# Attention outputs stored as high and low sums and added in the gating step, staging tiles laid out by last use, norm loads moved ahead, a minimum folded into the scores' reduction, and a dense store of the last block

## The chip, the cores and the metric

The kernel runs on one core of a Trainium2 chip. A core has a matrix engine (TensorE, PE in the profile; its weight loads are listed as PEld), three engines for elementwise work (VectorE is DVE, ScalarE is ACT, GpSimd is POOL), a queue that issues transfers (SyncE, SP), and 16 DMA engines between the chip's memory and the on-chip memory (SBUF; matmuls write to the accumulator memory, PSUM). The metric is the device time of one execution in microseconds (us), lower is better; three timed runs of the kernel before have a median of 1828.3 us (1823.72 to 1830.45).

## What is computed

Two layers over 2048 prompt frames and 32 frames of a second group, model width 1024, all in float32. Layer 0 is windowed attention in two kinds of head (A: 8 query heads that share 2 key/value heads, with sinks; B: 8 heads over a band of 9 chunks with a bias), each output gated by SiLU; layer 1 is a gated linear recurrence.

```python
for l in range(DEPTH):
    hp = rms_norm(yp, ln_pre[l])                      # and the same for the 32 frames
    if l % 2 == 0:
        qa, ka, va, ga, qb, kb, vb, gb = ab_project(hp, pos_p, w_in_ab[j])
        oa = prompt_band(qa, ka, va, N_PREV_A, None, sinks_a[j])
        ob = prompt_band(qb, kb, vb, N_PREV_B, relpos_b[j], None)
        mp = concatenate([oa * silu(ga), ob * silu(gb)]) @ w_out_ab
    else:
        mp = lru_mixer(hp, ...)       # in-projection, width-4 conv, gates, scan, out-projection
    yp = yp + rms_norm(mp, ln_post[l])
```

## The kernel before

**Numbers in two parts.** A float32 value is split into a high part that a fast matmul takes exactly and a low part, the rest. A dense product runs three matmuls for each 128 x 128 weight tile: high x high, high weight x low, low weight x high (`mm_list`). Attention's values are stored with the high part in columns 0 to 63 and the low part in columns 64 to 127 of one 128-wide tile, so that the product P V leaves the high sums on partitions 0 to 63 and the low sums on 64 to 127 of PSUM, and the two halves have to be added.

**Tiling.** The 2084 columns (2048 frames, 4 of padding, 32) are six blocks of 352 (the last has 324), taken in pairs b = 0, 1, 2; everything lies transposed, features on partitions. `dense_P` runs the input projection of layer 0: for each pair 26 weight tiles, each over both blocks. Its results are finished by small routines (`fin_ka`, `fin_q1`, `fin_v`, `fin_kq`, `fin_z`) that put keys, queries, values and gates into scratch tensors in the chip's memory. Attention runs beside it as units of 128 queries: `soft` does the scores, the minimum of their negative and the exponential, `transp` transposes the probabilities and splits them, then P V goes to the one tile of the ring `Or`. `evac_O` and `evac_B` bring that to SBUF (ScalarE copies one half, VectorE adds the other half to it; a head of kind B sums two more partial sums) and store it in the scratch tensor `oT` [1024, 2084]. `y_proc` loads `oT` and the gates `zT`, multiplies them and splits the product into `r0h`/`r0l` (pairs 0 and 2) or `r1h`/`r1l` (pair 1). From there `out_part` runs the output projection; its results pass `fin_out` (scale, squares, sum over features, reciprocal root, residual), into a tile `m`, and to `x2T`. Layer 1 then runs for each pair `norm_proc` (load `x2T`, norm, split), `in_part` (16 weight tiles with conv, gates and scan) and `out_part`; the last one writes the output `yT`.

**What sets the order.** The program is written out by a list scheduler inside the kernel (`Sched`, a cost for each operation, priorities in `spawn`). Each routine is a generator that yields a request (`R`) with the engine, what must be ready, and rings from which it wants tiles; where it asks for `("V", "G")` the scheduler takes VectorE or GpSimd, whichever it expects to finish first. So an edit in one routine reorders all engines behind it. After attention `sch.alone` keeps GpSimd out of most work.

**Places that the change touches.** `soft` (a row of up to 640 scores lies in two PSUM tiles, each reduced by one VectorE instruction into a column of `nm`, and a third instruction, `tensor_tensor(nm, nm, min)`, joins the two columns before the exponential); `evac_O`, `evac_B`; `y_proc` (12 quarter-block columns of 176, two half-feature loads each, ready for `out_part` a block at a time); the pool `stg` of staging tiles (`s`, `sr`, `vst`, `xcs`, `r0b`), whose place in SBUF is taken by the pool `mp` (`m`, `sacc`, `r`, `tz`) when the input projection is done, a new tile waiting for the last use of the ones under it; `dense_2`, which starts `norm_proc` of the next pair after `in_part`; `fin_out` with `res_load` for the last block, in two pieces of 162 columns, VectorE and GpSimd sharing the work.

Of the kernel before, what the change touches and what calls it, by code (L numbers as in the profile page):

```python
# [52 lines left out]
WIN = 3.4133  # L53

# [344 lines left out]
def hybrid_kernel(ctx, tc, I, O):  # L399
# [30 lines left out]
    oT, zT, x2T = dt("oT", [D, TOK]), dt("zT", [D, TOK]), dt("x2T", [D, TOK])  # L430
# [129 lines left out]
    def late_consts():  # L560
# [6 lines left out]
        SP.dma_start(out=oT[:, SEQ:S0].rearrange("(k p) t -> p k t", p=128), in_=zpad)  # L567
# [47 lines left out]
    def subs(blk):  # L615
        w = BW[blk] // 2
        return [(0, w), (w, w)]
# [46 lines left out]
    def norm_proc(src, b, gi, ri, key, rings, free=None, after=None, src_ready=(), then=None, blocks=(0, 1)):  # L664
# [119 lines left out]
    def y_proc(b, ri, key, free=None, then=None):  # L784

        hh, hl = RT[ri]
        todo = [(bi, t0, col, w, 4 * j) for bi, t0, col, w in cells_of(b) for j in range(2)]
        cur = {}

        def y_load():  # L790
            for n, (_, t0, _, w, k0) in enumerate(todo):
                g = xrr if b == 0 and n % 3 == 2 else xtr
                x, = yield R("SP", [("o", min(b + 1, 2)), ("z", b)], [g])
                for j, src in enumerate((oT, zT)):
                    SP.dma_start(out=x[:, 4 * j:4 * j + 4, :w],
                                 in_=src[k0 * 128:k0 * 128 + 512, t0:t0 + w].rearrange("(k p) t -> p k t", p=128))
                cur[n] = x, g
                sch.set((key, "x", n))
        spawn(y_load(), PY if b == 0 else PY2)
        for n, (bi, t0, col, w, k0) in enumerate(todo):  # L800
            yield R("V", [(key, "x", n)])
            x, g = cur[n]
            o = x[:, 0:4, :w]
            e, _ = yield R(("V", "G"), [x], cost=(0.8, 1.63))
            ENG[e].tensor_tensor(o, o, x[:, 4:8, :w], OP.mult)
            ks, cs = slice(k0, k0 + 4), slice(col, col + w)
# [5 lines left out]
            g.release(x)  # L812
            if n % 4 == 3:
                sch.set((key, bi), max(sch.t["V"], sch.t["G"]) + 0.13)
# [32 lines left out]
    sr = ring(sp, [128, BLK], "s", 7)  # L847
    srr = ring(sp, [128, 2, BLK], "sr", 3, F32R)
    hlr.append(srr)
    vsr = ring(sp, [128, 3, 2, 128], "vst", 1, F32R)  # L850

    xcr = ring(sp, [128, KT, 176], "xcs", 1)
    xct = {}
    ctn = {}
    r0[1] = sp.tile([128, BLK], F32, name="r0b", tag="r0b")
# [318 lines left out]
    otr = Ring(sch, ap, [128, 512], F32, "ot", 2, halves=True)  # L1174
# [56 lines left out]
    def soft(run, np_, groups, out, sink=None):  # L1231
# [10 lines left out]
        def reduce(ps, pieces, o0):  # L1242
            yield R("V", [ps] + ex)
# [7 lines left out]
            Sr.release(ps)  # L1251
            left[0] -= 1
# [9 lines left out]
        for gi, pieces in enumerate(groups):  # L1262
# [10 lines left out]
            spawn(reduce(ps, pieces, o0), PT)  # L1273
# [41 lines left out]
    def evac_O(b, ps, n, dst, view=None, beside=False):  # L1315

        m = 2 * n if beside else n
        ot, = yield R("A", [ps], [otr])
        x = ot.start_partition()
        A.copy(ot[:, :m], ps[64 - x:128 - x, :m])  # L1320
        yield R("V", [ot])
        V.tensor_tensor(ot[:, :m], ps[x:x + 64, :m], ot[:, :m], OP.add)
        Or.release(ps)
        if beside:
            yield R("V", [ot])
            V.tensor_tensor(ot[:, :n], ot[:, :n], ot[:, n:m], OP.add)
        yield R("SP", [ot])
        SP.dma_start(out=dst, in_=view(ot) if view else ot[:, :n])
        o_done(b, ot)

    def o_done(b, ot):
        otr.release(ot)
# [3 lines left out]

    def evac_B(b, ps, dst, i0):

        ot, = yield R("A", [ps], [otr])
        x = ot.start_partition()  # L1340
        v = ps.rearrange("p (i x c) -> p i x c", i=2, x=2)
        o = ot.rearrange("p (x i c) -> p i x c", i=2, x=2)
        A.copy(o[:, i0:], v[64 - x:128 - x, i0:])
        if i0:
            A.copy(o[:, 0, 1], v[64 - x:128 - x, 0, 1])
        yield R("V", [ot])
        V.tensor_tensor(o[:, i0:], v[x:x + 64, i0:], o[:, i0:], OP.add)
        if i0:
            V.tensor_tensor(o[:, 0, 1], v[x:x + 64, 0, 1], o[:, 0, 1], OP.add)
        Or.release(ps)  # L1350
        yield R("V", [ot])
        V.tensor_tensor(o[:, i0:, 1], o[:, i0:, 0], o[:, i0:, 1], OP.add)
        yield R("SP", [ot])
        SP.dma_start(out=dst, in_=ot[:, 256:512])
        o_done(b, ot)
# [4 lines left out]
    def run_B(b, h, tiles):  # L1360
# [7 lines left out]
        def unit(t):  # L1368
# [6 lines left out]
            def proc(run):  # L1375
# [35 lines left out]
                yield from evac_B(b, po, oT[512 + h * 64:512 + h * 64 + 64, ta * 128:ta * 128 + 256], 2 - len(edges))  # L1411
# [710 lines left out]
```

## Time and profile before

The profile is one execution, taken with every instruction's start and duration. It says:

| | |
|---|---|
| time of the profiled execution | 1823.5 us |
| its span, first to last instruction | 1821.7 us |
| median of three timed runs | 1828.3 us (1823.72 to 1830.45) |
| TensorE busy / VectorE / ScalarE / GpSimd | 95% / 85% / 55% / 18% of the span |
| DMA engines | 66.5% of 16, 362.80 MB, 199 GB/s |
| mean granted TensorE clock | 0.988 of full speed |
| matmuls of the dense projections | some 325 ns each, one starting about every 160 ns |

"Busy" counts an engine from an instruction's start to its end. Matmuls overlap: one is 320 ns under way, and the next starts 160 ns after it. So a PE that is idle in the records has had no matmul under way at all, and shorter delays between starts don't show as idle time. A row of a group gives engine, operation, output <- inputs, shape and count, then the summed time and the mean of one in ns, then the idle time of the engine just ahead of them and whose end closed it. All rows carry the line of one helper (L101), so groups are told apart by their tiles.

### The profile page before, as it was taken

The page shows a single profiled execution, that of the slowest core. Times are in us where ns is not written, and L with a number is a line of the kernel's source. Part 1 is how long each engine was busy: PE and PEld are TensorE (multiplying, and loading weights), DVE is VectorE, ACT ScalarE, POOL GpSimd, SP SyncE. Part 2 cuts the span into 40 slices and gives each one's busy share as a digit, 9 for nine tenths or more (in the row PEclk, how much of TensorE's full clock was granted, in tenths as well). Part 3 has the DMA queues.
Part 4 walks back from the last instruction along what each step waited for, and adds up shares of the span by engine and source line. Part 5 has one row for each costly group of instructions (what it writes and reads, how often), then busy time and mean ns, then how long its engine had stood idle before and what let it go on. Part 6 is the DMA issues. An engine that isn't in the chain of part 4 may idle for free.

```text
span 1821.7 us, 31694 instructions
## 1 busy us (share of the span) xinstructions
PE 1731.5 (95%) x11078; PEld 1671.8 (92%) x11078; DVE 1555.3 (85%) x3330; ACT 996.5 (55%) x2037; POOL 326.5 (18%) x284
## 2 busy tenths in 40 slices
PE   8999999999999999999998999998999999999995
PEld 7999999998999999899997999998999899999995
DVE  9899967899998779998988789899999988798843
ACT  4275543476666416665565344457753675447831
POOL 4332204323322233311222000000011000100002
PEclk8999999999999999999998999999999999999998
DMA  5788766888654368877764985684566735575376
GB/s 179 203 245 265 228 190 196 226 232 237 192 149 141 97 186 248 210 217 195 216 194 122 278 248 168 210 267 147 217 213 217 204 124 174 165 208 171 128 268 193
DMA packets 293576, 362.80 MB, mean 199 GB/s; under 512 B 36308, under 2 KB 244616, under 8 KB 293400
## 3 DMA queue, kind: packets, MB, share of 16 engines
q1 hardware_dynamic: 293416, 360.78, 66.5%
q8 instruction: 87, 1.43, 0.3%
q14 instruction: 73, 0.60, 0.1%
HBM read 255.77 MB, written 107.00 MB: 199 GB/s over the span
## 4 chain that ended last, share of the span: by engine, by line
PE 49%; DVE 29%; DMA 9%; ACT 6%; issue 4%; SPq 1%; POOL 1%; DVEq 0%; ACTq 0%; POOLq 0%
PE acc L101 35%; PE T L101 4%; PE O L101 4%; PE S L101 4%; DVE pt L101 3%; DVE ex L101 3%; DVE m L101 3%; DMA xr<-x2T 3%; DVE ss L101 2%; DVE ti L101 2%; DVE xs L101 2%; DVE s L101 2%; DVE pp L101 2%; DVE eti L101 1%; DVE wl L101 1%
## 5 line engine op out<-in xcount | busy, mean ns | idle before, releaser
L101 PE MATMUL acc<-r0h,wh 128*128 128x352 f32 (+2 forms) x1832 | 592.1, 323 | 6.7 <-ACT tzb L101 2.9
L101 PE MATMUL acc<-r0h,wl 128*128 128x352 f32 (+2 forms) x1832 | 592.2, 323 | 2.9 <-DMA wl<-wo1s 2.9
L101 PE MATMUL acc<-r0l,wh 128*128 128x352 f32 (+2 forms) x1832 | 592.5, 323 | 0.6 <-DVE r0l L101 0.5
L101 PEld LDWEIGHTS acc<-r0h,wh 128*128 128x128 f32 x1832 | 346.2, 189 | 9.3 <-ACT tzb L101 3.1
L101 PEld LDWEIGHTS acc<-r0h,wl 128*128 128x128 f32 x1832 | 346.3, 189 | 4.8 <-DMA wl<-wo1s 4.0
L101 PEld LDWEIGHTS acc<-r0l,wh 128*128 128x128 f32 x1832 | 346.4, 189 | 2.2 <-DVE r0l L101 1.2
L101 PE MATMUL acc<-r1h,wh 128*128 128x352 f32 (+1 forms) x864 | 277.5, 321 | 5.2 <-ACT tz L101 3.6
L101 PE MATMUL acc<-r1h,wl 128*128 128x352 f32 (+1 forms) x864 | 277.0, 321 | 1.6 <-DVE wl L101 1.6
L101 PE MATMUL acc<-r1l,wh 128*128 128x352 f32 (+1 forms) x864 | 276.9, 321 | 0.0
L101 ACT ACTIVATE pt<-pt,nm 128x256 f32<-128x256 f32 (+6 forms) x272 | 169.8, 627 | 61.2 <-DVE nm L101 59.3
L101 ACT CAST pp<-T 128x256 fp32r<-128x256 f32 (+4 forms) x314 | 134.0, 438 | 84.3 <-PE T L101 65.8
L101 PEld LDWEIGHTS acc<-r1h,wh 128*128 128x128 f32 x864 | 162.3, 188 | 6.4 <-ACT tz L101 4.5
L101 POOL TENSOR_SCALAR pt<-pt,rr 128x256 f32<-128x256 f32 (+4 forms) x142 | 100.2, 716 | 366.4 <-DVE rr L101 217.0
L101 PEld LDWEIGHTS acc<-r1h,wl 128*128 128x128 f32 x864 | 162.3, 188 | 1.9 <-DVE wl L101 1.9
L101 PEld LDWEIGHTS acc<-r1l,wh 128*128 128x128 f32 x864 | 162.3, 188 | 0.0
L101 PE MATMUL T<-ident,pt 128*128 128x128 f32 (+2 forms) x864 | 143.3, 274 | 18.0 <-DVE pp L101 10.2
L101 DVE TENSOR_TENSOR pp<-T,pp 128x256 fp32r<-128x256 f32 (+4 forms) x314 | 150.4, 496 | 7.9 <-ACT pp L101 6.0
L101 PE MATMUL O<-pp,vt 128*128 128x256 f32 (+3 forms) x728 | 135.9, 310 | 9.8 <-DVE pp L101 4.7
L101 PEld LDWEIGHTS T<-ident,pt 128*128 128x128 f32 (+2 forms) x864 | 101.7, 140 | 42.4 <-DVE pp L101 19.9
L101 DVE CUSTOM_DVE_ANT_0 pt<-S,bias 128x320 f32<-128x320 f32 (+2 forms) x240 | 108.8, 478 | 17.4 <-PE S L101 14.6
L101 PE MATMUL S<-kk,qa 128*128 128x320 f32 (+5 forms) x376 | 119.7, 333 | 3.8 <-DVE nm L101 3.3
L101 PEld LDWEIGHTS O<-pp,vt 128*128 128x128 f32 (+1 forms) x728 | 107.1, 193 | 16.0 <-DVE pp L101 6.1
(241 smaller groups left out, 3010.1 us busy)
## 6 DMA issues: line engine op xcount, KB each, us to landing
wst<-w_in SPq DMA_DIRECT2D x93, 512.0 KB, 4.4
wst<-wo_in SPq DMA_DIRECT2D x32, 512.0 KB, 5.6
wh<-w1s SPq DMA_DIRECT2D x32, 512.0 KB, 3.8
wl<-w1s SPq DMA_DIRECT2D x32, 512.0 KB, 4.6
wh<-wo1s SPq DMA_DIRECT2D x24, 512.0 KB, 3.9
wl<-wo1s SPq DMA_DIRECT2D x24, 512.0 KB, 4.7
kk<-kB SPq DMA_DIRECT2D x32, 320.0 KB, 4.8
vt<-vB SPq DMA_DIRECT2D x16, 640.0 KB, 4.8
```

The lines of the kernel that those rows point to most:

```text
L101: r = fn(*a, **k)
```

## The change

1. `oT` gets 2048 rows: high and low sums are stored as they come. `evac_O` (heads A) only copies on ScalarE, in two 128 x 256 pieces. `evac_add` (heads B and the 32 frames) adds the two partial sums at all 128 partitions, once. The add of high and low moves to `y_proc`, which now goes by two feature tiles of a whole block (352 columns): two loads of 64 partitions bring high and low side by side, one 128 x 704 add, one multiplication, copy and split, and a key for each feature tile, so that `out_part` can begin with the first.
2. The pool `stg` is laid out `r0b`, `vst`, `xcs`, `sr`, `s`; the second tile of `m` becomes `mb` and lies last in `mp`.
3. `norm_proc` of the next pair starts before `in_part`, loads at once, and holds its ScalarE work until `in_part` is written out.
4. The second reduction of a pair takes the first one's column of `nm` as its starting value, and the joining instruction goes.
5. The last block is finished in pieces of 176, 64 and 84 columns, its last matmuls split 240 + 84, all on VectorE, added into the residual's tile, and stored to a new output `yL` in which each partition's columns lie together; the host puts it in place.

```diff
-    oT, zT, x2T = dt("oT", [D, TOK]), dt("zT", [D, TOK]), dt("x2T", [D, TOK])
+    oT, zT, x2T = dt("oT", [2 * D, TOK]), dt("zT", [D, TOK]), dt("x2T", [D, TOK])
...
         early = len(rings) == len(idx)
         for i, g in zip(idx, rings):
             yield from load(i, g)
+        if hold:
+
+            yield R("A", [hold])
...
     def y_proc(b, ri, key, free=None, then=None):
-        todo = [(bi, t0, col, w, 4 * j) for bi, t0, col, w in cells_of(b) for j in range(2)]
+        todo = [(bi, T0[2 * b + bi], BW[2 * b + bi], k) for bi in range(2) for k in range(0, KT, 2)]
...
+                x, = yield R("SP", [("o", min(b + 1, 2))], [xtr])
+                for j in range(2):
+                    r = k * 256 + j * 256
+                    SP.dma_start(out=tile4(x)[j * 64:j * 64 + 64, :, :w], in_=oT[r:r + 256, t0:t0 + w].rearrange("(s d) t -> d s t", s=4))
...
             e, _ = yield R(("V", "G"), [x], cost=(0.8, 1.63))
-            ENG[e].tensor_tensor(o, o, x[:, 4:8, :w], OP.mult)
+            ENG[e].tensor_tensor(o, o, v[:, :, 1], OP.add)
+            th = sch.t[e] + 0.13
+            e, _ = yield R(("V", "G"), [lambda: th, z], cost=(0.8, 1.63))
+            ENG[e].tensor_tensor(o, o, tile4(z)[:, k % 4:k % 4 + 2, :w], OP.mult)
...
-            if n % 4 == 3:
-                sch.set((key, bi), max(sch.t["V"], sch.t["G"]) + 0.13)
+            for c in range(k, k + 2):
+                sch.set((key, bi, c), sch.t[e] + 0.13)
...
+                if sink is None:
+                    j = len(groups) - 1 - gi
                 V.tensor_tensor_reduce(out=pt[:np_, o0 + o:o0 + o + n], in0=ps[:np_, o:o + n], in1=bv, scale=-1.0,
-                                       scalar=BIG if sink is None else nsk[:np_, sink + j:sink + j + 1],
+                                       scalar=nsk[:np_, sink + j:sink + j + 1] if sink is not None else nm[:np_, 1:2] if on else BIG,
                                        op0=OP.add, op1=OP.min, accum_out=nm[:np_, j:j + 1])
...
-                if sink is None and len(groups) == 2:
-                    V.tensor_tensor(nm[:np_, 0:1], nm[:np_, 0:1], nm[:np_, 1:2], OP.min)
...
+    def evac_O(b, ps, g, t0):
+
+        for i in range(2):
+            ot, = yield R("A", [ps], [otr])
+            A.copy(ot, ps[:, i * 256:i * 256 + 256])
+            if i:
+                Or.release(ps)
+            yield R("SP", [ot])
+            SP.dma_start(out=o_two(g, i, t0, 128), in_=ot.rearrange("p (j n) -> p j n", j=2))
...
-        V.tensor_tensor(ot[:, :m], ps[x:x + 64, :m], ot[:, :m], OP.add)
-            V.tensor_tensor(ot[:, :n], ot[:, :n], ot[:, n:m], OP.add)
...
+            V.tensor_tensor(o2[:, i0:], v1[:, i0:], o2[:, i0:], OP.add)
...
-    mr, sar, r2r = ring(mp, [128, KT, BLK], "m", 2), ring(mp, [128, BLK], "sacc", 2), ring(mp, [128, BLK], "r", 1)
+    mr = ring(mp, [128, KT, BLK], "m", 1)
+    sar, r2r = ring(mp, [128, BLK], "sacc", 2), ring(mp, [128, BLK], "r", 1)
...
+                if half:
+
+                    V.tensor_tensor(xt[:, ks], m[:, ks, cc], xt[:, ks], OP.add)
+                    th = sch.t[e] + 0.13
+                    yield R("SP", [lambda: th])
+                    SP.dma_start(out=O["yL"][:, KT * o + ks.start * sw:KT * o + ks.stop * sw].rearrange("p (k t) -> p k t", t=sw), in_=xt[:, ks])
...
-                for o, sw in subs(2 * b + bi):
+                for o, sw in ((0, LAST[2][0]), LAST[2]):
```

Counted over the whole program, PE's matmuls stay as they are but for the last block's split; VectorE goes from 3314 to 3194 instructions, GpSimd from 255 to 207, ScalarE from 1672 to 1685, and SP from 1227 to 1277 transfers. The order is the same up to the first output of attention, some 98 us into the span. Three places on VectorE show what moved.

VectorE inside attention, before: the second reduction of a row of scores (ISA, from the score tile `S` with the bias into `pt` and the column `nm`), its read-out, the joining of the columns, and an output of a B head between them (`ot` from PSUM tile `O`, later `ot` with itself):

```order
L101 ISA pt_210,nm_216<-S_195,bias_208 128x320
L101 ISA nm_216 128x1
L101 TENSOR_TENSOR nm_216<-nm_216 128x1
L101 TENSOR_TENSOR ot_215<-O_198,ot_215 64x2x2x128
L101 TENSOR_TENSOR pp_213<-T_196,pp_213 128x3x128
L101 ISA pt_211,nm_218<-S_194,bias_208 128x320
L101 ISA nm_218 128x1
L101 TENSOR_TENSOR ot_215<-ot_215 64x256
```

The same engine in such a place of the changed kernel, from the scaling of a unit's probabilities on:

```order
L103 TENSOR_SCALAR pt_209<-pt_209,rr_227 32x544
L103 TENSOR_TENSOR ot_215<-O_198,ot_215 128x256
L103 ISA pt_211,nm_221<-S_194,bias_208 128x320
L103 ISA nm_221 128x1
L103 ISA pt_211,nm_221<-S_195,bias_208,nm_221 128x320
```

One output instruction of 128 x 256 stands for the two of 64 partitions, `nm` has become an input of the second reduction, and the row `nm <- nm` is gone.

VectorE near the last outputs of attention, before: `ot` and `pp` are attention's, `sacc` and `wh` belong to the output projection of layer 0 (`sacc` gathers its squares):

```order
L101 TENSOR_TENSOR ot_214<-O_198,ot_214 64x2x2x128
L101 TENSOR_TENSOR ot_214<-ot_214 64x256
L101 TENSOR_TENSOR pp_212<-T_196,pp_212 128x3x128
L101 TENSOR_TENSOR pp_212<-T_197,pp_212 128x3x128
L101 TENSOR_TENSOR sacc_10372<-sacc_10372,tz_10375 128x352
L101 TENSOR_TENSOR pp_212<-T_196,pp_212 128x2x128
L101 TENSOR_TENSOR pp_212<-T_197,pp_212 128x2x128
L101 CAST wh_120<-wst_117 128x1024
```

The changed kernel at the last output of attention: `s` <- `s`, `acc` is the gate of an input projection (`fin_z`), `r0l` and the two rows of `xt` are `y_proc`'s split, add and multiplication:

```order
L103 TENSOR_TENSOR pp_212<-T_196,pp_212 128x2x128
L103 TENSOR_TENSOR r0l<-xt_151,r0h 128x2x352
L103 TENSOR_TENSOR r0l<-xt_152,r0h 128x2x352
L103 TENSOR_TENSOR ot_215<-O_198,ot_215 128x256
L103 SCALAR_TENSOR_TENSOR s_187<-s_187,acc_158 128x352
L103 CAST wh_119<-wst_117 128x1024
L103 TENSOR_TENSOR wl_122<-wst_117,wh_119 128x1024
L103 SCALAR_TENSOR_TENSOR s_189<-s_189,acc_159 128x324
L103 TENSOR_TENSOR xt_151<-xt_151 128x2x352
L103 CAST wh_120<-wst_118 128x1024
L103 TENSOR_TENSOR xt_151<-xt_151,xr_153 128x2x352
```

Before, attention reached into the output projection; now its last output stands ahead of the last gates of the input projection. On PE, 76 matmuls of the input projection (4 of 352 columns, 72 of 324) come behind attention's last one, and then the 384 of pair 0's output projection without any attention between them; before, 92 of those 384 stood among attention's and none of the input projection's came after it.

VectorE at the end of the program, before (`r` is the reciprocal root, `m` the scaled result, `xt` the residual):

```order
L101 RECIPROCAL r_10374<-r_10374 128x162
L101 TENSOR_TENSOR m_10371<-m_10371,r_10374 128x5x162
L101 RECIPROCAL r_157<-r_157 128x162
L101 TENSOR_TENSOR m_10371<-m_10371,r_157 128x5x162
L101 TENSOR_TENSOR m_10371<-m_10371,xt_151 128x3x162
L101 TENSOR_TENSOR m_10371<-m_10371,xt_152 128x3x162
```

And in the changed kernel, from the last reciprocal on:

```order
L103 RECIPROCAL r_157<-r_157 128x84
L103 TENSOR_TENSOR mb_10441<-mb_10441,r_10439 128x5x64
L103 TENSOR_TENSOR mb_10441<-mb_10441,r_10439 128x3x64
L103 TENSOR_TENSOR mb_10441<-mb_10441,r_157 128x5x84
L103 TENSOR_TENSOR mb_10441<-mb_10441,r_157 128x3x84
L103 TENSOR_TENSOR xt_152<-mb_10441,xt_152 128x880
L103 TENSOR_TENSOR xr_153<-mb_10441,xr_153 128x320
L103 TENSOR_TENSOR xr_153<-mb_10441,xr_153 128x420
L103 TENSOR_TENSOR xt_152<-mb_10441,xt_152 128x528
L103 TENSOR_TENSOR xr_153<-mb_10441,xr_153 128x192
L103 TENSOR_TENSOR xr_153<-mb_10441,xr_153 128x252
```

What GpSimd did beside VectorE before (four of the eight large operations) is now VectorE's, in more and smaller pieces, with the residual's tile as the output that is stored.

More of the change, by code (lines that the diff above doesn't have):

```diff
@@ L566, in late_consts @@
         V.tensor_scalar(nsk, sk, -1.0, None, OP.mult)
-        SP.dma_start(out=oT[:, SEQ:S0].rearrange("(k p) t -> p k t", p=128), in_=zpad)
+        for x in range(2):
+            SP.dma_start(out=oT[x * D:(x + 1) * D, SEQ:S0].rearrange("(k p) t -> p k t", p=128), in_=zpad)
         V.tensor_scalar(hba, vec[:, BA], 0.5, None, OP.mult)
@@ L662, in norm_sum, with norm_proc @@
         return ps
-    def norm_proc(src, b, gi, ri, key, rings, free=None, after=None, src_ready=(), then=None, blocks=(0, 1)):
+    def norm_proc(src, b, gi, ri, key, rings, free=None, after=None, src_ready=(), then=None, blocks=(0, 1), hold=None):
         if after is not None:
@@ L1173, in hybrid_kernel @@
     sch.cuts.update((x[2].tensor.name, (2560, 1280)) for x in ppr.idle)
-    otr = Ring(sch, ap, [128, 512], F32, "ot", 2, halves=True)
+    otr = ring(ap, [128, 256], "ot", 4)
     nmr, smr, rr4 = ring(ap, [128, 4], "nm", 4), ring(ap, [128, 4], "ssm", 4), ring(ap, [128, 4], "rr", 4)
@@ L1240, in soft, with reduce @@
         o0 = 0
-        def reduce(ps, pieces, o0):
-            yield R("V", [ps] + ex)
+        def reduce(ps, pieces, o0, gi):
+            on = gi > 0 and sink is None
+            yield R("V", [ps] + ex + ([(uid, 0)] if on else []))
             o = 0
@@ L1272, in soft @@
                 o += n
-            spawn(reduce(ps, pieces, o0), PT)
+            spawn(reduce(ps, pieces, o0, gi), PT)
             o0 += o
@@ L1410, in proc @@
                 run.v_done(2)
-                yield from evac_B(b, po, oT[512 + h * 64:512 + h * 64 + 64, ta * 128:ta * 128 + 256], 2 - len(edges))
+                yield from evac_add(b, po, out[:, :, 0], out[:, :, 1], [o_head(8 + h, ta * 128, 256)], 2 - len(edges))
             return proc
@@ L1486, in proc @@
             run.v_done()
-            yield from evac_O(2, po, DEC, oT[512 + h * 64:512 + h * 64 + 64, S0:TOK], beside=True)
+            yield from evac_add(2, po, po[:, DEC:2 * DEC], po[:, :DEC], [o_head(8 + h, S0, DEC)])
         return Run(with_cache(need(2, (6 + 3 * p, 7 + 3 * p, 8 + 3 * p))),
@@ L1509, in proc @@
             run.v_done()
-            yield from evac_O(2, po, 128, oT[g * 256:(g + 1) * 256, S0:TOK].rearrange("(j d) n -> d j n", j=4),
-                              lambda ot: ot[:, :128].rearrange("d (j n) -> d j n", j=4), True)
+            yield from evac_add(2, po, po[:, 128:256], po[:, :128], [o_two(g, i, S0, DEC) for i in range(2)])
         return Run(with_cache(need(2, (0, 1, 3 + 2 * g))),
@@ L1626, in __init__ @@
             self.m = self.sa = None
-            self.n, self.left = 0, 2
+            self.cells = LAST if final and bi else subs(2 * b + bi)
+            self.n, self.left = 0, len(self.cells)
     def fin_out(S, c, acc, rel, cs):
@@ L1653, in fin_out @@
         m, half = S.m, S.final and S.bi == 1
-        pieces = [(o, sw) for o, sw in subs(blk) if cs.start <= o < cs.stop]
+        pieces = [(o, sw) for o, sw in S.cells if cs.start <= o < cs.stop]
         xg = xtr if S.final else xrr
@@ L1712, in res_load @@
         S.xt, S.xk = {}, {}
-        for o, sw in subs(2 * S.b + S.bi):
+        if S.cells is LAST:
+            xa, = yield R("SP", rings=[xtr])
+            xb, = yield R("SP", rings=[xrr])
+            at = 0
+            for o, sw in LAST:
+                x = xb if o else xa
+                S.xt[o] = x.rearrange("p k t -> p (k t)")[:, at:at + KT * sw].rearrange("p (k t) -> p k t", k=KT)
+                at = at + KT * sw if o else 0
+                x_load(S.xt[o], S.residual, T0[2 * S.b + S.bi] + o, sw)
+                S.xk[o] = sch.dma_end
+            return
+        for o, sw in S.cells:
             xt, = yield R("SP", rings=[S.xg])
@@ L1955, in dense_2 @@
         for b in range(3):
-            yield from out_part(b, base + 8 * b, b % 2, I["xT"], LN_POST, x2T, lambda k, bi, b=b: (("y", b), bi), late_m=b > 0)
+            yield from out_part(b, base + 8 * b, b % 2, I["xT"], LN_POST, x2T, lambda k, bi, b=b: (("y", b), bi, k), late_m=b > 0)
             if b == 0:
@@ L2099 @@
     c = np.ascontiguousarray
-    yT = g["yT"]
+    yT = np.concatenate([g["yT"]] + [g["yL"][:, KT * o:KT * (o + w)].reshape(128, KT, w).transpose(1, 0, 2).reshape(1024, w) for o, w in LAST], 1)
     def kT(x, h, n):
```

123 lines of the change are left out of this document (66 added, 57 removed).

## The prediction

> **What bounds the kernel now.** I read the shares first, then the windows by stage.
>
> ```profile
> PE 1731.5 (95%) x11078; PEld 1671.8 (92%) x11078; DVE 1555.3 (85%) x3330; ACT 996.5 (55%) x2037; POOL 326.5 (18%) x284
> ```
>
> PE has work under way 95% of the span and none of the change takes matmuls away, so a gain can only come out of PE's idle time, delays between its starts, and the two ends. The windows (start:end, length, then busy time of PE, PEld, DVE, ACT, POOL, granted clock, DMA share, GB/s) say where those lie.
>
> ```profile
> 98.00:400.00 302.00, 295.61 (x1911) 284.36 (x1910) 258.93 (x652) 161.30 (x430) 81.85 (x84) 1.00 0.77 223
> 400.00:700.00 300.00, 288.60 (x1936) 277.46 (x1935) 261.62 (x692) 166.91 (x376) 89.65 (x77) 0.99 0.63 178
> 700.00:940.00 240.00, 233.66 (x1615) 220.56 (x1614) 216.10 (x682) 150.65 (x391) 54.46 (x56) 1.00 0.77 210
> 940.00:1003.00 63.00, 55.45 (x358) 52.08 (x357) 52.32 (x135) 35.91 (x79) 22.95 (x13) 0.92 0.49 141
> 1003.00:1049.00 46.00, 46.00 (x291) 46.00 (x290) 32.51 (x44) 16.96 (x33) 0.94 (x1) 1.00 0.95 287
> 1049.00:1183.00 134.00, 125.38 (x779) 123.69 (x778) 118.11 (x167) 61.45 (x106) 0.00 (x0) 0.99 0.73 209
> 1183.00:1736.00 553.00, 533.72 (x3289) 522.34 (x3288) 493.02 (x742) 347.33 (x500) 21.75 (x14) 1.00 0.57 185
> ```
>
> Attention beside the input projection lasts from 98 to 940 us; PE idles 6.4 + 11.4 + 6.3 = 24.1 us there. Its end, 940 to 1003, idles 7.6 us more at a clock of 0.92, which costs 63 x 0.08 = 5 us. In both DVE is the fullest engine after PE: 789 of 905 us, 87%. The waits of PE from 98 to 940 (output, who ended the wait, total, times, longest) name it:
>
> ```profile
> PE T L101 <- DVE pp L101: 6.9, 12, 2.1
> PE O L101 <- DVE ot L101: 2.7, 2, 2.0
> PE T L101 <- DVE rr L101: 2.6, 2, 2.4
> PE O L101 <- DVE pp L101: 2.1, 3, 1.1
> PE T L101 <- DVE pt L101: 1.8, 3, 1.2
> PE S L101 <- DVE nm L101: 1.6, 2, 0.9
> ```
>
> These six sum to 17.7 us. Attention is the stage that DVE relief can shorten, and only by what PE now loses there.
>
> **The change, part by part.** Minimum and outputs first, with DVE's groups from 98 to 1003 (count, then busy us and mean ns):
>
> ```profile
> L101 DVE TENSOR_TENSOR ot<-O,ot 64x512 f32<-64x512 f32 x79 | 54.2, 686 | 11.1 <-ACT ot L101 10.0
> L101 DVE TENSOR_TENSOR wl<-wst,wh 128x1024 fp32r<-128x1024 f32 x39 | 51.5, 1321 | 0.8
> L101 DVE CUSTOM_DVE_ANT_0 pt<-S,amask,nsk 128x256 f32<-128x256 f32 x108 | 46.4, 478 | 2.9 <-PE S L101 2.5
> L101 DVE TENSOR_TENSOR pp<-T,pp 128x256 fp32r<-128x256 f32 x104 | 42.2, 415 | 1.8 <-ACT pp L101 0.9
> L101 DVE TENSOR_TENSOR nm<-nm 128x1 f32<-128x1 f32 x96 | 30.8, 321 | 3.3
> L101 DVE TENSOR_SCALAR pt<-pt,rr 128x640 f32<-128x640 f32 x39 | 24.5, 633 | 0.7
> L101 DVE TENSOR_TENSOR ot<-ot 64x256 f32<-64x256 f32 x47 | 23.9, 509 | 0.7
> L101 DVE TENSOR_SCALAR pt<-pt,rr 128x256 f32<-128x256 f32 x50 | 22.3, 500 | 0.2
> L101 DVE TENSOR_TENSOR xt<-xt 128x704 f32<-128x704 f32 x5 | 5.4, 1079 | 0.9 <-DMA xt<-zT 0.9
> L101 DVE CUSTOM_DVE_ANT_0 pt<-S,bias 128x256 f32<-128x256 f32 x8 | 3.3, 414 | 0.0
> ```
>
> The 96 joins go: -30.8 us, 0.32 each for a single column. Part of that is standing still, as in this stretch of the timeline (start, duration, engine, operation):
>
> ```profile
> 957.56 2.36 POOL L101 TENSOR_TENSOR wl<-wst,wh 128x1024 fp32r<-128x1024 f32 x1
> 958.07 0.08 DVE L101 DVE_READ_ACCUMULATOR2_ANT nm<- 128x1 f32 x1
> 958.18 1.75 DVE L101 TENSOR_TENSOR nm<-nm 128x1 f32<-128x1 f32 x1
> 960.32 0.44 PE L101 MATMUL T<-ident,pt 128*128 128x128 f32 x2 [1.66 <-DVE pp L101]
> ```
>
> The join lasts until GpSimd's split ends, and PE loses 1.66 us. Such a stall can pass to the next DVE instruction with both operands in SBUF, so it isn't all won. Against it: a reduction with a column as its start costs 478 - 414 = 64 ns more (x96, +6.1), and the second reduction, which now starts beside the first one's read-out, must await it: 0.08 us (the read-out) to twice that, I take 0.12, +11.5. Outputs: the two `ot` rows, 54.2 + 23.9 = 78.1 us, go; 48 adds of 128 x 256, priced as the `pp` row with its one PSUM operand, take 48 x 0.415 = 19.9. (The narrower forms of both are left out; they favour the change by less than 10.) Eight adds of pair 0's gating come back, 8 x 1.08 = 8.6. And the scheduler, finding DVE freer, takes 20 scalings of 128 x 640, 15 of 128 x 256 and 9 splits `wl` from GpSimd by its order: 12.7 + 7.5 + 11.9 = +32.1. Net: -30.8 + 6.1 + 11.5 - 78.1 + 19.9 + 8.6 + 32.1 = -30.7, so DVE goes from 789 to 758 us of 905, 84%. ScalarE's copies in more pieces are covered: it is busy 515 of 905 us. The gain for PE is bounded by 0 (DVE's share hardly falls, and latencies stay) and -24.1 (all idle time to 940). I take half of the 17.7, **-9**, since seven tenths of what DVE gives up (78.1 of 108.9 us) is filled again and the stalls behind GpSimd fall with GpSimd's work.
>
> Handover, 940 to 1003: before, 7.6 us idle and 5 of clock, 12.6 lost. After, the last output stands ahead of the last gates, and 76 input-projection matmuls and then the output projection are all PE has. The rows of DVE's order from the last `ot` to the eighth split sum to 22.9 us by their durations; PE has 76 + 24 to 48 matmuls, 0.16 us apart, before the last of these is due, 16 to 20 us. So 3 to 7 us idle, plus one load behind the last store, 5.2 us by the row below: some 10, **-2** against 12.6. Ends: -8 (loads hidden) and +15 (items one by one, the rival below).
>
> Transfers (size, median us to landing):
>
> ```profile
> kk<-kB SPq DMA_DIRECT2D x32, 320.0 KB, 4.8
> vt<-vB SPq DMA_DIRECT2D x16, 640.0 KB, 4.8
> xt<-oT SPq DMA_DIRECT2D x12, 352.0 KB, 5.2
> oT<-ot SPq DMA_DIRECT2D x32, 128.0 KB, 4.8
> oT<-ot SPq DMA_DIRECT2D x64, 64.0 KB, 3.2
> yT_out<-m SPq DMA_DIRECT2D x2, 405.0 KB, 6.2
> ```
>
> `kk` fills 64 partitions and moves half the bytes of `vt`, which fills 128, in the same 4.8 us; the new gating loads are of 64 partitions. The Trainium skill, "SBUF — State Buffer", section "Can I just issue two DMAs to hit both halves?", says two transfers at partitions 0 and 64 together gain only 6% over one, because they serialize. The two rows agree that 64 partitions are slow for their size; that a pair serializes no run here shows. By that rule a pair takes 2 x 4.8 = 9.6 us instead of 5.2 (an estimate by that page), and the handover would come to about +2 instead of -2. The sum stays with 5.2.
>
> The other 16 adds, 16 x 0.97 = 15.5 us, fall behind attention, where DVE is free for 46 - 32.5 + 134 - 118.1 = 29.4 us. There `out_part` already stops when a finished tile is late:
>
> ```profile
> 1078.28 0.43 PE L101 MATMUL acc<-r1h,wh 128*128 128x352 f32 x1 [2.13 <-ACT tz L101]
> ```
>
> **+2**, from 0 to +8 (half of the adds end on that chain). Stored twice, `oT` brings 8.5 MB more written and read at a DMA share of 0.5 to 0.8: 0, up to +3. Early norm loads: layer 1 idles 553 - 533.7 = 19.3 us in all, little of it named for a load: **-1**, from -4 to 0. Staging by last use: one wait that I can name,
>
> ```profile
> 970.86 0.55 ACT L101 ACTIVATE m<-acc,vec 128x352 f32<-128x352 f32 x1 [0.95 <-DMA zT<-s]
> ```
>
> **-1**, from -2 to 0.
>
> Tail. From the last dense matmul:
>
> ```profile
> 1804.73 0.28 PE L101 MATMUL acc<-r0h,wl 128*128 128x162 f32 x1
> ...
> 1812.17 2.07 DVE L101 TENSOR_TENSOR m<-m,xt 128x486 f32<-128x486 f32 x1
> 1813.75 0.94 SPq L101 DMA_DIRECT2D yT_out<-m  x2
> ```
>
> DVE ends 9.5 us after it; the last issue ends at 1814.7, the span 7.0 later. After, DVE does all eight operations in pieces of 64 and 84 columns, 9.2 us by the rows above scaled with width: nothing won. The last store falls from 405 KB to 252 x 128 x 4 B = 129 KB: 3.2 to 4.8 us instead of 7.0. **-3.5** with one issue less in the way, from -5 to 0.
>
> Sum: -9 - 2 + 2 - 1 - 1 - 3.5 = -14.5, so 1823.5 - 14.5 = 1809.0 by the profiled execution. That one lies 4.8 us below the median of 1828.3, by which it would be 1813.8. I forecast **1811**.
>
> **Rivals.**
> - *More comes out of attention*: delays between starts, which the idle time doesn't count, shrink with DVE's share. For: 87% on DVE throughout. Against: seven tenths of the relief is used up again. With -20 instead of -9: 1800.
> - *Handed back at the handover*: PE arrives earlier, but pair 0's gating waits for the last output, and items come as loads, add, product, cast and split one after another. For: the reordering. With +11 instead of -2: 1824.
> - *Slower*: the eight gating items come two at a time. Their load of 5.2 and four operations of 1 us make 9.2 us a pair, 37 us for eight, behind a store's 4.8, against 12 + 8 us of PE's work: 22 us idle, and another 5 of lowered clock as in the row at 0.92. With +27 instead of -2 that is 1840. It decides from some 24 us lost there instead of 12.6. Against: pair 0's first items stand ahead of the last `ot`.
> - *It doesn't do what it says*: PE's waits pass from `nm` and `ot` to other DVE work, as the scheduler fills DVE again. With 0 instead of -9 and the tail alone: 1820 to 1825.
>
> **How the numbers follow.** Forecast 0.50 (own range 1803 to 1819), more 0.16, handed back 0.20, no effect 0.07, slower 0.07. A measurement of this kernel tells about 0.5%, 9.1 us, from no change; faster by more means under 1819.2: forecast and more, 0.66. Within: handed back and no effect, 0.27. Slower: 0.07. For 8 in 10 the range leaves out the slower case and the ends of the outer ones: 1793 to 1828.
>
> **What would show it.** Right: DVE under 85% from 98 us to the end of attention, no `nm` from `nm`, fewer PE waits that DVE's `pp` and `ot` end, attention's last matmul some 9 us earlier, under 12 us lost behind it, under 4 us from the last issue to the end. Wrong: PE's waits for DVE as before; a hole of over 15 us ahead of the first output projection, ended by `r0l`; more waits for `tz` and `m` behind it; a tail of 17 us.

## The result

The changed kernel takes 1844.25 us, median of four runs (1842.51 to 1850.02), against 1826.26 us of the kernel before on the same chip (1823.72 to 1830.45). The ratio is 1.0093 with a 95% interval of 1.0071 to 1.0115: it is 0.9% slower, where I had forecast 1811 us. The profiled execution has a span of 1843.3 us, 21.6 more than before. Two of the runs below hold one disturbed execution each (e3 one of 1911.6 us at a clock of 0.84; e16 its profiled one, of 4294.5 us, so that it has no usable trace), which the ratios leave out and which moves the medians by under 1 us.

The page of the changed kernel, shares of the span, and its windows from attention to the first input part of layer 1, cut where its stages end (pair 0's output projection at 1061, all three at 1200, the input part at 1352):

```profile
PE 1747.0 (95%) x11078; PEld 1686.4 (91%) x11078; DVE 1518.2 (82%) x3210; ACT 969.6 (53%) x2058; POOL 260.5 (14%) x218
```

```profile
98.00:400.00 302.00, 295.30 (x1904) 284.02 (x1903) 254.60 (x636) 154.55 (x440) 64.36 (x61) 1.00 0.80 233
400.00:700.00 300.00, 292.40 (x1977) 282.34 (x1977) 249.14 (x664) 158.42 (x388) 63.02 (x54) 1.00 0.68 188
700.00:940.00 240.00, 231.51 (x1603) 216.90 (x1602) 195.09 (x641) 146.94 (x413) 47.02 (x42) 0.99 0.82 221
940.00:1003.00 63.00, 46.47 (x280) 42.07 (x278) 39.30 (x79) 20.83 (x46) 7.91 (x5) 0.84 0.74 199
1003.00:1061.00 58.00, 57.03 (x340) 56.38 (x340) 40.08 (x52) 22.04 (x40) 0.00 (x0) 0.94 0.99 258
1061.00:1200.00 139.00, 130.03 (x786) 128.05 (x786) 120.94 (x169) 63.50 (x111) 0.00 (x0) 0.96 0.83 221
1200.00:1352.00 152.00, 140.55 (x835) 137.36 (x834) 141.16 (x202) 103.94 (x133) 0.00 (x0) 0.96 0.61 200
```

VectorE is freer, as meant: 254.6 + 249.1 + 195.1 = 698.8 us from 98 to 940, against 736.7 before. PE gets almost nothing of it: it idles 6.7 + 7.6 + 8.5 = 22.8 us there, against 24.1. Then the loss begins: from 940 to 1003 it idles 16.5 us instead of 7.6, and the granted clock is 0.84, 0.94, 0.96 and 0.96 in four stretches that had 0.92, 1.00, 0.99 and 1.00. By stages, pair 0's output projection ends 13 us later than before (1061.6 against 1048.6), pairs 1 and 2 take 3.5 us more, the first input part of layer 1 takes 152.6 us against 144.3, and all that comes later together 3 us less. These make the 21.6.

What PE waits for from 98 to 940:

```profile
PE T L103 <- DVE pp L103: 4.4, 9, 1.3
PE O L103 <- ACT ot L103: 2.6, 3, 1.2
PE O L103 <- DMA vt<-vA: 2.5, 1, 2.5
PE O L103 <- DMA vt<-vBs: 2.4, 2, 1.6
PE T L103 <- DVE pt L103: 1.7, 5, 0.5
PE O L103 <- DMA vt<-vAs: 1.6, 1, 1.6
...
PE T L103 <- DVE rr L103: 0.7, 1, 0.7
PE S L103 <- DVE nm L103: 0.7, 1, 0.7
PE O L103 <- DVE ot L103: 0.6, 2, 0.5
...
PE O L103 <- DVE pp L103: 0.5, 1, 0.5
```

The six waits for DVE that summed to 17.7 us sum to 8.6. In their place stand loads of values (`vt`, 6.5 us) and ScalarE's copies of the outputs (2.6 us).

The loss at the handover, seen on PE and on DVE (start, duration, operation, in brackets idle time before it and what ended it):

```profile
981.62 0.32 PE L103 MATMUL acc<-r0h,wl 128*128 128x352 f32 x1
986.91 0.66 PE L103 MATMUL acc<-r0h,wh 128*128 128x352 f32 x1 [4.97 <-ACT r0h L103]
987.84 0.66 PE L103 MATMUL acc<-r0l,wh 128*128 128x352 f32 x1 [0.27 <-DVE r0l L103]
988.29 0.49 PE L103 MATMUL acc<-r0h,wl 128*128 128x352 f32 x1
988.59 0.49 PE L103 MATMUL acc<-r0h,wh 128*128 128x352 f32 x1
```

```profile
984.23 0.89 DVE L103 TENSOR_TENSOR ex<-ex 128x704 f32<-128x704 f32 x1 [3.41 <-DMA ex<-oT]
...
997.84 0.89 DVE L103 TENSOR_TENSOR xt<-xt 128x704 f32<-128x704 f32 x1 [6.59 <-DMA xt<-oT]
```

PE waits for ScalarE's `r0h`, that for DVE's add, and the add for its load. Behind the hole matmuls start 0.30 us apart, no longer 0.16: each hole is paid a second time in clock. And DVE, which has GpSimd's share of the work too from here on (GpSimd is idle from 1003 to 1352 us), stands still in its written order with everything behind the add. Its waits from 960 to 1200 us, first of the changed kernel, then of the kernel before:

```profile
DVE ex L103 <- DMA ex<-oT: 15.2, 7, 3.9
DVE xt L103 <- DMA xt<-oT: 9.2, 4, 6.6
...
DVE wh L103 <- DMA xt<-oT: 2.5, 1, 2.5
```

```profile
DVE wh L101 <- DMA xt<-zT: 1.2, 1, 1.2
```

27 us against 1. The DMA engines, from 960 to 1061 us:

```profile
q1 hardware_dynamic: 17837, 25.36, 96.6%
...
ex<-oT SPq DMA_DIRECT2D x22, 352.0 KB, 7.5
xt<-oT SPq DMA_DIRECT2D x14, 352.0 KB, 7.7
```

They are full, and a load of 352 KB, now on 64 partitions, takes 7.5 us where one on 128 took 5.2 before.

### The profile page after: what moved, and what is told of

Read it like the earlier page. It is cut to its first block, busy times and chain, and to the rows that moved or that the text cites. A ratio compares the mean times of both kernels' runs of the same rounds, so it can differ in the third digit from the quotient of the medians.

```text
span 1843.3 us, 31660 instructions
## 1 busy us (share of the span) xinstructions
PE 1747.0 (95%) x11078; PEld 1686.4 (91%) x11078; DVE 1518.2 (82%) x3210; ACT 969.6 (53%) x2058; POOL 260.5 (14%) x218
## 5 line engine op out<-in xcount | busy, mean ns | idle before, releaser
L103 ACT CAST pp<-T 128x256 fp32r<-128x256 f32 (+5 forms) x314 | 134.1, 440 | 76.5 <-PE T L103 69.5
L103 DVE TENSOR_TENSOR pp<-T,pp 128x256 fp32r<-128x256 f32 (+5 forms) x314 | 150.0, 499 | 9.6 <-ACT pp L103 9.1
L103 PE MATMUL O<-pp,vt 128*128 128x256 f32 (+3 forms) x728 | 132.9, 307 | 11.5 <-ACT ot L103 2.6
L103 DVE TENSOR_TENSOR wl<-wst,wh 128x1024 fp32r<-128x1024 f32 (+1 forms) x97 | 121.0, 1247 | 8.3 <-ACT wh L103 6.0
L103 POOL TENSOR_SCALAR pt<-pt,rr 128x256 f32<-128x256 f32 (+4 forms) x94 | 66.4, 713 | 349.1 <-DVE rr L103 196.7
```

Source lines behind the costliest of these rows:

```text
L103: r = fn(*a, **k)
```

## Experiments

My theory after the result (A): the gating loads come late and DVE and PE wait for them, so part 1 makes the loss. Rival (B): the other parts, above all the early norm loads. Times are medians; a ratio is to the kernel before on the same chip.

**Parts undone and alone.** The first four runs: the diff without part 1; part 1 alone; gating loads in one transfer; the diff without part 3. The edit of the third:

```diff
-                for j in range(2):
-                    r = k * 256 + j * 256
-                    SP.dma_start(out=tile4(x)[j * 64:j * 64 + 64, :, :w], in_=oT[r:r + 256, t0:t0 + w].rearrange("(s d) t -> d s t", s=4))
+                SP.dma_start(out=tile4(x)[:, :, :w], in_=oT[k * 256:k * 256 + 512, t0:t0 + w].rearrange("(s p) t -> p s t", p=128))
...
-            SP.dma_start(out=o_two(g, i, t0, 128), in_=ot.rearrange("p (j n) -> p j n", j=2))
+            for x in range(2):
+                SP.dma_start(out=o_two(g, i, t0, 128)[x], in_=ot[x * 64:x * 64 + 64].rearrange("p (j n) -> p j n", j=2))
```

> The changed kernel with its first part undone: outputs of attention are joined and stored as before, gating goes by quarter blocks; staging order, early norm loads, joined minimum and dense last store stay. Theory A (the gating items of pair 0 come late behind attention, and that and the lowered clock behind the holes make most of the 18 us): PE's waits for r0h and r0l ahead of the first output projection fall from 17.5 us to under 5, the stretch from 940 us to the end of pair 0's output projection is again some 108 us long, and the time is 1815 to 1828 us. Theory B (the other four parts make it, above all the early norm loads that hold engines in the first input part of layer 1): the time stays at 1836 us or more and that part stays at 150 us or longer.

Measured: 1815.72 us, ratio 0.9947 (0.9930 to 0.9963): faster than before and 28.5 us faster than the whole change. So part 1 makes the loss, as A says; that it does so by its loads is left to the next runs. It is also a kernel that beats both.

> The kernel before with the first part alone (high and low sums stored, added in the gating step). Theory A: the handover loss is all there, over 13 us of waits of PE for r0h and r0l, TensorE clock under 0.9 in the 60 us around it, and the time is 1836 to 1850 us. Theory B: 1822 to 1831 us.

Measured: 1858.76 us, 1.0191 (1.0157 to 1.0226). A again, and worse than expected: 34 us alone. Here too PE waits for the gating (13.9 us for `r0h`), and a hole of 12.8 us, ended by DVE's `xs`, stands in the first input part of layer 1.

> The changed kernel with the rows of the scratch tensor so ordered that one transfer of 128 partitions brings high and low sums of two feature tiles (704 KB) instead of two of 64 partitions (352 KB each); the stores go as two of 64 partitions. If loads on 64 partitions are what makes the items late: the load of an item lands within 7 us, PE's waits for r0h and r0l ahead of the first output projection fall from 17.5 us to under 9, and the time is 1828 to 1837 us. If it is the chain load, add, product, cast, split behind the last outputs with too few tiles, or the bytes themselves: the waits stay above 13 us and the time at 1840 to 1850 us.

Measured: 1848.22 us, 1.0126 (1.0077 to 1.0175). The trace answers one way and the time another. The one load of 704 KB lands sooner than each of the pair did with 352, at 81% of the DMA engines instead of 97 (its transfers from 960 to 1061 us):

```profile
q1 hardware_dynamic: 19776, 26.40, 81.1%
...
xt<-oT SPq DMA_DIRECT2D x11, 704.0 KB, 6.2
```

PE's waits for `r0h` and `r0l` fall from 17.5 to 9.3 us. But in this kernel, which has twice as many stores, attention ends later (its last product starts at 991.7 us, not 961.6; that the stores cause it isn't shown), and a new hole of 10.3 us opens at the head of layer 1, ended by DVE's `r1l`. So pairs on 64 partitions make the loads slow, but this remedy loses elsewhere as much as it brings. On the rule quoted in the prediction (the Trainium skill, "SBUF — State Buffer", "Can I just issue two DMAs to hit both halves?"): the direction agrees, 6.2 us for one of 704 KB against 7.5 and 7.7 us for each of two; its 6%, and that a pair serializes, isn't tested here, as other transfers run beside them.

> The changed kernel without its third part: the norm of the next pair starts after the input part, as before. If the early loads and what they hold make the first input part of layer 1 longer (152 us against 144 before): that part falls to 147 us or less and the time to 1834 to 1840 us. If that part is long because the work left over from the gating and the output projections, and the clock behind the holes, reach into it: it stays at 149 us or more, and the time at 1841 to 1850 us.

Measured: 1857.38 us, 1.0179 (1.0145 to 1.0213), above both ranges. The first input part stays at 152.8 us, so the early loads don't lengthen it. They were worth 13 us, at a place that I hadn't looked at: without them PE waits 16.4 us at the head of the *second* input part.

**What in part 1 costs.** Half of the bytes; the store and the norm alone; the minimum alone.

```diff
-                    SP.dma_start(out=tile4(x)[j * 64:j * 64 + 64, :, :w], in_=oT[r:r + 256, t0:t0 + w].rearrange("(s d) t -> d s t", s=4))
+                    SP.dma_start(out=tile4(x)[j * 64:j * 64 + 64, ::2, :w], in_=oT[r:r + 128, t0:t0 + w].rearrange("(s d) t -> d s t", s=2))
...
-            ENG[e].tensor_tensor(o, o, v[:, :, 1], OP.add)
+            ENG[e].tensor_tensor(o, o, o, OP.add)
```

> The changed kernel, but each of the two 64-partition loads of a gating item brings only half of its rows (176 KB instead of 352), and the add takes the loaded half twice; the low sums are left out of the result. The number of transfers, the engines' operations and the order of attention stay. If the bytes of the gating loads, which fill the DMA engines to 97 to 100% from 960 to 1061 us, are what makes the items late: loads land in under 5 us, PE's waits for r0h and r0l ahead of the first output projection fall from 17.5 to under 9 us, and the time is 1828 to 1838 us. If the chain of an item and its two tiles set the pace: the waits stay above 13 us and the time at 1840 us or more.

Measured: 1834.78 us, 1.0051 (1.0027 to 1.0075); the waits for `r0h` and `r0l` are 12.7 us, between the two. DVE's waits for these loads fall from 27 to 8 us. Bytes are a part, some 8 to 10 us (by the ratios and by the medians), not all.

> The kernel before with the fourth part alone (the second reduction starts from the first one's column, no joining instruction). If DVE's joins and the stalls behind GpSimd in them cost PE time in attention: the end of pair 0's output projection comes 4 to 8 us earlier than at 1048.6 us and the time is 1816 to 1822 us. If PE's waits only pass to other work: 1822 to 1829 us.

Measured: 1840.51 us, 1.0076 (1.0046 to 1.0105): neither. Attention ends as before (pair 0's output projection at 1051.0 us), but at the head of the second input part stands the hole of e4:

```profile
1402.47 0.43 PE L101 MATMUL misc<-xs,onesr 128*128 128x352 f32 x1 [1.07 <-DVE xs L101]
1419.31 0.66 PE L101 MATMUL acc<-r1h,wh 128*128 128x352 f32 x1 [16.40 <-ACT r1h L101]
```

```profile
1396.39 1.34 DVE L101 SCALAR_TENSOR_TENSOR xt<-xt,vec,ss 128x176 f32<-128x176 f32 x4
...
1409.52 1.69 DVE L101 TENSOR_TENSOR m<-m,r 128x880 f32<-128x880 f32 x2
1411.13 1.33 DVE L101 SCALAR_TENSOR_TENSOR xt<-xt,vec,ss 128x176 f32<-128x176 f32 x4
```

The scheduler put 13 us of the last tile's finishing between two steps of the next pair's norm on DVE. An edit in attention moved work 400 us later.

> The kernel before with the fifth part alone (last block in pieces of 176, 64 and 84 columns, all on DVE, dense store). From the last dense matmul to the end 12 to 14.5 us instead of 17.0, the time 2.5 to 5 us under that of before. If the store's landing is no shorter: 16 to 18 us, no difference.

Measured: 1817.96 us, 0.9955 (0.9935 to 0.9975). From the last dense matmul to the end 12.5 us instead of 17.0, as expected. That is 4.5 of the 7.4 us; the rest came earlier and I have no cause for it.

> The kernel before with the third part alone (norm of the next pair started before the input part, its ScalarE work held). My sum has 1 us for it. In the changed kernel it is worth 13 us (1857.4 without it against 1844.3). If that worth belongs to the kernel in general: 1812 to 1818 us here. If it only covers a hole that other parts make: 1820 to 1828 us, and no hole of over 5 us at the head of the second input part of layer 1 either way.

Measured: 1833.78 us, 1.0039 (1.0023 to 1.0056), slower than either case. Alone they cost time, in no single hole; why stays open.

**What the relief is worth, and where the rest goes.** e9 is the diff without the hunks of `y_proc` and its keys. e10 drops the add. e11 is parts 2, 3 and 5, e12 the diff without part 4.

```diff
-            e, _ = yield R(("V", "G"), [x], cost=(0.8, 1.63))
-            ENG[e].tensor_tensor(o, o, v[:, :, 1], OP.add)
-            th = sch.t[e] + 0.13
-            e, _ = yield R(("V", "G"), [lambda: th, z], cost=(0.8, 1.63))
+            e, _ = yield R(("V", "G"), [x, z], cost=(0.8, 1.63))
             ENG[e].tensor_tensor(o, o, tile4(z)[:, k % 4:k % 4 + 2, :w], OP.mult)
```

> The changed kernel with attention's outputs stored as high and low sums, but the gating step of before: quarter blocks, four feature tiles to an item, no add. The low sums are never loaded and the rows are not those of the right heads, so that part is left out of the result. It keeps DVE's relief in attention and takes away everything that the gating adds. If the relief is worth something to PE by itself (my term of 9 us): 1800 to 1810 us against 1815.7 with the outputs of before, and the end of pair 0's output projection earlier than 1042 us. If PE's waits only pass from DVE to loads and ScalarE's copies: 1811 to 1822 us.

Measured: 1800.68 us, 0.9869 (0.9850 to 0.9888). The relief is real: 15 us against e1 by the medians, and pair 0's output projection ends at 1035.2 us (e1: 1042.5, before: 1048.6). The two traced executions differ by only 8.7 us, 7.3 of them up to that point. And e9 joins high and low nowhere, so this is what the relief is worth before its price. Its windows:

```profile
98.00:940.00 842.00, 823.64 (x5519) 787.61 (x5517) 704.50 (x1956) 463.22 (x1247) 176.05 (x157) 1.00 0.76 215
940.00:1003.00 63.00, 60.05 (x381) 58.82 (x382) 48.10 (x82) 29.05 (x59) 7.75 (x5) 0.97 0.76 236
```

From 98 to 1003 PE idles 21.3 us instead of 31.7 before, with DVE busy 752.6 of 905. The gating of the changed kernel costs 44 us against this one.

> The changed kernel without the 24 adds of high and low in the gating step (left out of the result; loads, tiles and all else stay). If these adds (21 us of DVE) make the late items and the backlog behind them: the first input part of layer 1 falls from 152 to 147 us or less and the time to 1832 us or less. If the loads set the pace: 1838 to 1846 us, PE's waits for r0h and r0l ahead of the first output projection above 13 us.

Measured: 1853.56 us, 1.0144 (1.0102 to 1.0186), above both ranges, with one of four runs, the traced one, at 1839.7. Too wide to tell it from the changed kernel, but no gain: no cost of the adds shows. DVE waits 33 us for gating loads here, and the first input part takes 151.8 us against 152.6.

> The kernel before with parts two, three and five: staging order, early norm loads, dense last store, without the outputs and without the joined minimum. If the joined minimum is worth 4 us or more in attention: 1819 to 1825 us (against 1815.7 with it). If it is worth nothing: 1812 to 1818 us.

> The changed kernel with the joining instruction of before. If the joined minimum helps in attention: 1847 to 1856 us. If it is worth nothing or only reorders: 1838 to 1847 us.

Measured: 1823.08 us, 0.9987 (0.9966 to 1.0007), and 1856.07 us, 1.0174 (1.0147 to 1.0201). In company the joined minimum brings 7 us (e1 against e11) and 12 us (the change against e12).

**Form or loads, first pair or all.** e13 loads half the rows by one transfer and has no add; e14 joins the outputs of the first six query tiles as before and gates pair 0 with the code of before:

```diff
+                r = k * 256
+                SP.dma_start(out=tile4(x)[:, ::2, :w], in_=oT[r:r + 256, t0:t0 + w].rearrange("(s p) t -> p s t", p=128))
```

```diff
+        if b == 0:
+            yield from y_proc0(b, ri, key, free, then)
+            return
...
+                if t < 6:
+                    yield from join_O(b, po, g, t)
+                else:
+                    yield from evac_O(b, po, g, t * 128)
```

> The changed kernel with its new form of gating items (two feature tiles of a block, gates in another tile, ready by feature tile), but only half the rows are loaded, by one transfer of 128 partitions (352 KB, as before), and there is no add; the low sums are left out of the result and the rows are not those of the right heads. If the form of the items (two tiles each, a longer chain for the first) sets the pace: 1822 to 1840 us, PE's waits for r0h and r0l above 9 us. If the second load and the 64 partitions do: 1798 to 1808 us, near the 1800.7 us of the old gating, and those waits under 5 us.

Measured: 1829.14 us, 1.0013 (0.9996 to 1.0030). The handover is healed: the waits for `r0h` and `r0l` are 3 us, loads land in 4.5 us, pair 0's projection ends at 1042.2 us. The time is not, because of two holes behind it (PE's waits from 1042 to 1250 us):

```profile
PE g L103 <- DVE wl L103: 10.5, 2, 9.2
PE g L103 <- DVE gl L103: 7.4, 1, 7.4
```

These are DVE's splits of weights, late in its written order though no load holds it up. So 15 of the 44 us go when the second load, the 64 partitions and the add are taken away together. The other 28 to e9 are 21.6 between the two traced executions: 7 lie ahead of the end of pair 0's projection (1042.2 against 1035.2) and 14.6 behind it, where DVE's order differs. Whether the form of the items forces that order, or a better one was near, isn't settled.

> The changed kernel, but the outputs that pair 0's gating needs (the first six query tiles) are joined and stored as before, and pair 0 is gated as before by quarter blocks without an add; pairs 1 and 2, which load while the output projection of pair 0 runs, keep the new outputs and gating. Nothing is left out. If only the first pair's gating items are late on PE's path: PE's waits for r0h and r0l ahead of the first output projection fall under 5 us, pair 0's output projection ends by 1045 us and the time is 1805 to 1822 us. If the loads of pairs 1 and 2, which crowd the DMA engines at the same time, make the loss, or their backlog at the first input part of layer 1: 1828 to 1845 us.

Measured: 1861.69 us, 1.0186 (1.0164 to 1.0208), above both ranges. PE has no wait for `r0h` or `r0l` ahead of the first output projection, which ends at 1048 us, and yet the kernel is the slowest of all: pairs 1 and 2 take 169 us where they took 135 before. (To make room for the joined outputs it also has two `ot` tiles instead of four, so more than pair 0 differs.) DVE's waits from 960 to 1200 us and PE's from 1040 to 1250:

```profile
DVE ex L103 <- DMA ex<-oT: 20.3, 7, 5.6
```

```profile
PE misc L103 <- DVE xs L103: 15.3, 5, 7.1
PE g L103 <- DVE r0l L103: 11.0, 2, 10.0
PE acc L103 <- DVE r1l L103: 10.1, 1, 10.1
```

The loads of pairs 1 and 2, which I had taken to be covered by pair 0's projection, stop DVE as well, and PE runs into what DVE has left undone; how much of the 169 us is theirs isn't separated.

**The other parts in good company.** e15 is e1 without part 3, e16 is e1 without part 2.

> The kernel of e1 (all but the outputs) without the early norm loads: staging order, joined minimum, dense last store. With the minimum alone (e6) a hole of 16.4 us stood at the head of the second input part of layer 1, ended by ScalarE's r1h, and the same hole came in e4; no run with early norm loads has it. If the norm of the next pair is simply late whenever it isn't loaded early and the order before it has moved: that hole is here again, over 10 us, and the time is 1825 to 1836 us. If the hole came by chance of the order in those two kernels: no such hole, 1812 to 1820 us.

Measured: 1828.73 us, 1.0009 (0.9991 to 1.0027), with the 16.4 us hole, ended by `r1h`, for the third time. The early norm loads are worth 13 us where the joined minimum is; without the minimum no such hole stands there (before, e2, e7).

> The kernel of e1 with the staging order of before: early norm loads, joined minimum, dense last store. My sum has 1 us for the staging order. If it is that little: 1813 to 1820 us. If the order of the staging tiles frees the tiles m and sacc for the first output projection in time: 1822 us or more, with longer waits of ScalarE's m and tz between 1003 and 1120 us.

Measured: 1819.22 us, 0.9950 (0.9931 to 0.9969), 3.5 us above e1 with intervals that overlap: little, and not told apart.

## Why the prediction was wrong, by its steps

**Attention, -9: the relief came, and was given away.** The prices held. The second reduction with a start value takes 549 ns against 486, 63 more where I had 64, and DVE idles 10.2 us before the 96 of them, where I had 11.5 for the wait; an output's add takes 416 ns where I had 415 (groups from 98 to 1003 us):

```profile
L103 DVE CUSTOM_DVE_ANT_0 pt<-S,bias,nm 128x320 f32<-128x320 f32 x96 | 52.7, 549 | 10.2 <-DVE nm L103 0.7 <-PE acc L103 0.5 <-PE S L103 0.3
L103 DVE CUSTOM_DVE_ANT_0 pt<-S,bias 128x320 f32<-128x320 f32 x96 | 46.6, 486 | 19.8 <-PE S L103 19.4
...
L103 DVE TENSOR_TENSOR ot<-O,ot 128x256 f32<-128x256 f32 x48 | 20.0, 416 | 3.6 <-DMA oT<-ot 2.1 <-ACT ot L103 1.0
```

PE's waits for DVE fell by 9.1 us, from 17.7 to 8.6. But only 1.3 of it showed in PE's idle time; the waits for `vt` and for copies took the rest. With the old gating, and with no add of high and low anywhere, the relief brings 15 us by the medians (e9 against e1), 7.3 of them seen up to the end of pair 0's projection: near what I took from the profile, for a kernel that doesn't pay for it.

**Handover, -2: the step that failed.** I priced it with one load of 5.2 us behind the last store, and the items as DVE work. Measured are 9 us of idle time more instead of 2 less, plus clock: 13 us to the end of pair 0's projection, where my end for the term was +15. PE waited for `r0h` and `r0l` again and again, not once: 17.5 us in 11 waits. The row of 5.2 us was of loads on 128 partitions. Full DMA engines alone don't make 7.5 of it, for before the change they were nearly as busy from 1003 to 1049 us (94%), and there such loads landed in 5.4 and 5.7 us:

```profile
q1 hardware_dynamic: 15643, 13.16, 94.2%
...
ex<-oT SPq DMA_DIRECT2D x6, 352.0 KB, 5.7
...
xt<-oT SPq DMA_DIRECT2D x6, 352.0 KB, 5.4
```

What the change adds is twice the bytes of `oT` on half the partitions, in the hundred microseconds where most of the 24 items load, and bytes loaded to 64 partitions keep the engines busy longer. From 960 to 1061 us the rate at full busy share (MB moved, over 101 us and the share) is 246 to 260 GB/s in all six traces with such pairs of loads (the change, e2, e4, e10, e12, e14), 289 with half of each (e5), and 295 to 322 in the ten that load `oT` on 128 partitions (before and the others). I had the sign in hand, `kk` on 64 partitions as slow as `vt` with twice its bytes, and kept 5.2 in the sum. Nor would a dearer load alone have done, as the term put a single one on the path. I had written 0 for "stored twice", by a mean share of 0.5 to 0.8 over long stretches. The rival that I called slower had the place and the row of items that PE waits for, and 0.07. That its 1840 us lie near is partly luck: it took +27 for the handover alone, where pair 0's projection ends 13 us later, and the rest of the way came from stages that it doesn't mention. What I held against it, that pair 0's first items stand ahead of the last output, was true of two items of eight.

**Gating adds, +2: wrong thing priced.** The adds cost nothing that can be seen (e10). What they wait for does: 27 us in which DVE stands in its written order. (The two aren't one to one: e5 has 8 us of such waits and gains some 8 to 10.) I asked whether DVE had room for 15.5 us of adds (29 us free) and not what is queued behind an add whose load is late. e14 shows such a loss apart from pair 0. The first input part of layer 1, 8.3 us longer, had no term at all. It is long in every trace with the new gating (149.6 us in e13, 155.7 in e5, 161.7 in e3) and short with the old (143.3 in e9, 145.3 in e1), also where DVE waits little for loads, so the loads alone don't make it. What does stays open.

**Norm loads, -1:** mis-sized. They cover a norm that the joined minimum's order makes late: 13 us in two pairs of runs (the change against e4, e1 against e15), and e6 has the same hole. Alone they cost 8 us.

**Staging, -1:** not contradicted (e16). **Tail, -3.5:** right, -4.5:

```profile
1830.75 0.29 PE L103 MATMUL acc<-r0h,wl 128*128 128x84 f32 x1
...
1838.66 0.69 DVE L103 TENSOR_TENSOR xr<-mb,xr 128x192 f32<-128x192 f32 x2
1839.34 1.16 SPq L103 DMA_DIRECT2D yL_out<-xr  x2
```

DVE ends 8.6 us after the last dense matmul (I had 9.2), and the span 2.8 us after the last issue, where it was 7.0.

So the four parts without the outputs bring 0.5%, and the outputs take it back three times over.

## To carry to other kernels

When an edit moves work off a full engine and into a later step, price the later step's loads in the form and number that the edit gives them, with all that moves in that stretch, not at the median landing of before. An engine with a fixed order stops with everything behind the one instruction whose load is late, as VectorE did here for 27 us: ask that of each new load, also where PE seems covered. And where a scheduler writes the program, a part tried alone tells little of its worth in company (the minimum: 15 us lost alone, 7 to 12 won with early norm loads), so undo parts of the whole as well as trying them singly.

## Not expected of the hardware

A hole on PE costs beyond itself: behind holes of 5.0 and 7.4 us the granted clock was 0.50, from 987 to 1009 us, with matmuls starting 0.30 us apart, and 1.00 again from 1012:

```profile
987.00:993.00 6.00, 4.76 (x12) 3.24 (x12) 3.37 (x4) 0.78 (x1) 0.00 (x0) 0.50 1.06 372
...
1006.00:1009.00 3.00, 3.00 (x12) 3.00 (x11) 2.21 (x3) 2.33 (x4) 0.00 (x0) 0.50 0.96 254
...
1012.00:1016.00 4.00, 4.00 (x27) 4.00 (x26) 1.62 (x3) 0.91 (x2) 0.00 (x0) 1.00 1.10 219
```

From 940 to 1352 us the four windows make 63 x 0.16 + 58 x 0.06 + 139 x 0.04 + 152 x 0.04 = 25 us of missing clock, where those of before make 6 (63 x 0.08 + 134 x 0.01). That is a bound and not the loss, as much of it lies in the holes, where PE has nothing to do: from 987 to 1009 us it was busy 12.1 of 22 us, and by an estimate from these rows its 33 matmuls there, 0.14 us further apart, lost 4.6 us and not 11.
